# FoX attention: scaling by one over the row sums moved from the probabilities to the gate

## The chip, the cores and the metric

The kernel runs on one core of a Trainium2 chip. The metric is the device time of one execution in microseconds (us), where lower is better. One core has five engines that each work through their own list of instructions in order: TensorE (PE; its weight loads are listed as PEld), VectorE (DVE), ScalarE (ACT), GpSimd (POOL) and SyncE (SP, which here only starts DMAs). ACT starts DMAs too.

## The reference, cut to what matters

Two decoder layers on 1024 tokens of width 1024, in float32. Each layer feeds one projection of the normalised input to three mixers. The one that changes is FoX, a causal softmax attention with a forget decay (8 heads of 64), followed by a SiLU gate and a branch projection:

```python
def _fox_attention(q, k, v, log_f):
    c = jnp.cumsum(log_f, axis=1).transpose(0, 2, 1)
    for s0 in range(0, s, Q_BLOCK):                       # Q_BLOCK = 128
        logits = einsum('bhqd,bhkd->bhqk', q[s0:s1], k[:s1]) * scale
        logits = logits + c[:, :, s0:s1, None] - c[:, :, None, :s1]
        p = jax.nn.softmax(jnp.where(_causal_mask(s0, s1), logits, -jnp.inf), axis=-1)
        outs.append(jnp.einsum('bhqk,bhkd->bhqd', p, v[:, :, :s1]))
...
    y_fox = _fox_attention(...) * jax.nn.silu(fg)
    y_diff = _diff_attention(...) * jax.nn.silu(dg)       # 4 heads, two softmax maps each
    y_conv = cb * _short_conv(cc * cx, conv_w) * jax.nn.silu(cg)
    m = (gates[:, :, 0] * (y_fox @ w_fox) + gates[:, :, 1] * (y_diff @ w_diff)
         + gates[:, :, 2] * (y_conv @ w_conv))
    return x + _rmsnorm(m @ w_o, post_g)
```

## The kernel before, in words

A layer is a row of stages. Projections for the convolution and for most gates come first and keep TensorE full. Then come the attention windows: four FoX pairs of heads, then four differential heads. Each window has attention units as its main work and a list of "fills" beside it (`PLAN`): projections for later heads (tile F on TensorE), gates, and in the last two windows the preparation of the FoX output (`y_prep`, four chunks of 128 rows) and the first three chunks of the branch projection (`merge_br`, "br"). The merge and the output projection follow.

A FoX unit is one head and two query blocks of 128 (`fox_unit`). Stage 1 computes negated logits on TensorE into tile S (L783, L784, with the causal guard L787). DVE adds the decay row cB and finds the minimum (L847, written as ISA in the order and as CUSTOM_DVE in the trace). ACT takes the exponential and its row sum (L854). DVE takes one over the sum (L857) and multiplies the whole probability block by it (L858). Stage 2 (`pv_group`) transposes the probabilities on TensorE into tile T (L174), ACT copies the upper part to tile pt (L821), DVE subtracts for the lower part (L822), and TensorE accumulates P V in tile O (L893, L894). ACT and DVE evict O (L903, L900), and a DMA writes it to the DRAM tensor `of`. Stage 1 of a unit is issued one unit ahead of stage 2.

`y_prep` loads a chunk of attention output o and of gates g, multiplies them on DVE (L1038), and splits the product yf into an upper part on ACT (L1043) and a lower part on POOL (L1044). The branch product reads yf on TensorE (L351 to L353).

What the other engines do after a step is put into the program by an estimated clock (`Clock.later`), and a list scheduler with its own cost model then fixes each engine's order, all but SP's, which follows the program. Large SBUF tiles come from one pool of 41 blocks (`blk`); an SP load into a block waits until the block is free, and everything behind it in SP's queue waits with it.

Of the kernel before, what the change touches and what calls it, by code (L numbers as in the profile page):

```python
# [11 lines left out]
F32 = mybir.dt.float32  # L12
# [4 lines left out]
ALU = mybir.AluOpType  # L17
# [3 lines left out]
S = 1024  # L21
D = 1024
P = 128
HD = 64
EPS = 1e-6
# [9 lines left out]
# order of the query blocks (pairs) of a head, and of the FoX heads (pairs)  # L35
G_ORDER = (1, 2, 3, 0)
FOX_ORDER = (2, 3, 0, 1)
# work on the tensor engine that runs beside each attention pair or head
# [12 lines left out]
# weights of the attention's steps when work beside it is spread between them  # L51
W1F, W2F, W1D, W2D = 0.188, 1.324, 0.31, 1.574
# PSUM banks: logits, transposes, outputs, work beside the attention
# [3 lines left out]
def mm_us(n):  # L57
    """Time of a pass of n columns through the tensor engine."""
    return max(n, 128) * 0.000417


class Clock:
    """Estimated time of the tensor engine. What the other engines do after one of its steps is emitted
    when its turn would come, beside later steps, so that no engine's queue waits on an early entry."""
# [57 lines left out]
def interleave(main, main_cost, fill, fill_cost):  # L122
    """Emit the steps of main with those of fill spread evenly between them."""
# [12 lines left out]
class Trunk:  # L136
# [35 lines left out]
    def transpose(self, out, x):  # L172
        """One block of 128 x 128, through the tensor engine."""
        self.nc.tensor.transpose(out, x, self.ident)  # L174
# [88 lines left out]
    def emit_load(self, key, kt, nco, eng):  # L263
        """DMA one weight tile [P, kt*nco] and split it into hi + lo float32r parts."""
# [18 lines left out]
    def load_w(self, key, kt, nco, eng="gpsimd"):  # L283
        """The next weight tile; the loads of the tiles after it are issued ahead of its use."""
# [19 lines left out]
    def emit_pair(self, l, i0, i1):  # L304
        """DMA two 128-column weight chunks, b1j and b2j their upper and lower halves, and form the split
        operands of a Strassen-Winograd step: b11, b21 | b12 - b11 (t1), b21 - t2 (t4) |
        b22 - t1 (t2), b22 - b12 (t3) | b22."""
# [38 lines left out]
    def mm3(self, ps, pairs, start=True, stop=True):  # L346
        """Accumulate the products of split operands: lo*hi + hi*lo + hi*hi for each k tile."""
# [7 lines left out]
    def proj_g(self, w, h):  # L355
        """One 128-column chunk of the input projection, transposed, for token half h."""
# [18 lines left out]
    # ------------------------------------------------------------------ norm  # L375
    def rstd(self, ss, scale):
        """(ss * scale + EPS) ** -0.5 per partition."""
# [9 lines left out]
    def hk(self, h, k, o=0, n=512):  # L387
        """Tokens o..o+n of a half of hT, 128-row tile k: hi and lo."""
        return [t[:, k % 2, o:o + n] for t in self.hT[h][k // 2]]

    def norm_rows(self, xs, gB, hT, tb0, step):
        """rmsnorm of blocks of 128 tokens (rows of the tiles xs), transposed and split into hT."""
# [40 lines left out]
    # ------------------------------------------------------------------ Strassen-Winograd  # L433
    def build_s(self, L):
        """Sums of the quadrants of h (tokens x features), split: s1 = a21 + a22, s2 = s1 - a11,
        s3 = a11 - a21, s4 = a12 - s2. a21 itself waits in DRAM meanwhile."""
# [46 lines left out]
    def strassen(self, L, c0, c1, use, uv=None):  # L483
        """Two chunks of the input projection, transposed, with seven products in place of eight.
        use(j, h, x, ps, own): chunk j, token half h is x + ps; x may be overwritten if own."""
# [19 lines left out]
    def plain(self, L, jobs):  # L505
        """Chunks of the input projection, transposed, [(chunk, use)]; the first token half of three
        comes before the second."""
# [8 lines left out]
    def total(self, x, ps, own):  # L516
        """x + ps in SBUF, or ps as it is."""
# [6 lines left out]
    # ------------------------------------------------------------------ conv  # L524
    def conv_pair(self, L, c, nplain):
        """Chunks c, c + 1 of the convolution branch; the first nplain projections without Strassen."""
# [785 lines left out]
```

## Time and profile before

| Quantity | Value |
|---|---|
| Time, three runs | 2569.18, 2570.14 (median), 2570.54 us |
| The profiled execution, first to last instruction | 2573.8 us |
| TensorE busy | 2439.4 us, 95% of the span |
| VectorE busy | 1699.8 us, 66% |
| ScalarE busy | 1109.0 us, 43% |
| GpSimd busy | 838.9 us, 33% |
| FoX windows, layer 0 and layer 1 | 587 to 845 us and 1868 to 2126 us |

The profile is of one execution. A wait in it is put down to the instruction that ended last before the waiting one started. Idle time matters where it is TensorE that idles. In the windows view the numbers behind an engine are its busy time and, in brackets, its instructions.

### The profile page before, as it was taken

What the parts mean: (1) busy time and instruction counts of PE and PEld (TensorE: products, weight loads), DVE (VectorE), ACT (ScalarE), POOL (GpSimd) and SP (SyncE); (2) the same over time, 40 slices, a digit from 0 to 9 for tenths busy, and PEclk for the clock granted to TensorE, in tenths of its full rate; (3) what the DMA queues carried; (4) which work ended last, traced back from release to release, by engine and by line L of the source; (5) the groups of instructions that cost most, each with busy time, mean ns of one, the idle gap of its engine ahead of it and who ended that gap; (6) DMA issues with size and microseconds to landing.
All of it is one profiled execution on the core that took longest, in us unless ns stands there. A gap on an engine that the chain in (4) does not pass through costs nothing. (4 is left out here: it accounts for less than half of the span.)

```text
span 2573.8 us, 35788 instructions
## 1 busy us (share of the span) xinstructions
PE 2439.4 (95%) x13104; PEld 2051.8 (80%) x13104; DVE 1699.8 (66%) x3017; ACT 1109.0 (43%) x2282; POOL 838.9 (33%) x605
## 2 busy tenths in 40 slices
PE   7899999999999999899997999999999999989998
PEld 6677888888978778778976778888888787877798
DVE  6976464447687777767578654344486878777664
ACT  4224333336554554543433232233365545555333
POOL 1566334421112222361025652344211122232600
PEclk9899999999999999999998999999999999999999
DMA  4012223332222222563521122233321222225534
GB/s 167 33 50 95 92 96 111 107 132 70 63 69 68 63 87 64 169 220 129 194 90 41 50 95 89 75 117 130 93 80 53 69 68 75 82 70 186 202 119 180
DMA packets 111808, 260.35 MB, mean 101 GB/s; under 512 B 15744, under 2 KB 40576, under 8 KB 111632
## 3 DMA queue, kind: packets, MB, share of 16 engines
q1 hardware_dynamic: 56304, 183.33, 20.7%
q10 hardware_dynamic: 55328, 74.73, 9.4%
q8 instruction: 104, 1.70, 0.3%
q14 instruction: 72, 0.59, 0.1%
HBM read 183.48 MB, written 55.64 MB: 93 GB/s over the span
## 5 line engine op out<-in xcount | busy, mean ns | idle before, releaser
L279 POOL TENSOR_TENSOR wlo<-wraw,whi 128x1024 fp32r<-128x1024 f32 (+2 forms) x93 | 198.5, 2135 | 628.1 <-ACT whi L276 442.3
L351 PE MATMUL F<-ht,wlo 128*128 128x512 f32 x792 | 331.1, 418 | 0.0
L353 PE MATMUL F<-ht,whi 128*128 128x512 f32 x792 | 318.5, 402 | 0.0
L352 PE MATMUL F<-ht,whi 128*128 128x512 f32 x792 | 317.0, 400 | 0.0
L319 POOL TENSOR_TENSOR wlo<-sw,whi 128x512 fp32r<-128x512 f32 x160 | 224.6, 1414 | 228.6 <-ACT whi L318 203.1
L319 POOL TENSOR_TENSOR wlo<-wraw,whi 128x1024 fp32r<-128x1024 f32 x80 | 159.3, 1992 | 188.1 <-ACT whi L318 187.9
L318 ACT CAST whi<-sw 128x512 fp32r<-128x512 f32 x160 | 96.1, 619 | 245.6 <-DVE sw L321 106.1
L353 PEld LDWEIGHTS F<-ht,whi 128*128 128x128 f32 x792 | 150.8, 190 | 30.6
L276 ACT CAST whi<-wraw 128x1024 fp32r<-128x1024 f32 (+2 forms) x126 | 118.0, 939 | 129.8 <-PE F L353 41.9
L822 DVE TENSOR_TENSOR pt<-T,pt 128x512 fp32r<-128x512 f32 (+1 forms) x240 | 147.4, 632 | 37.4 <-ACT pt L821 35.7
L351 PEld LDWEIGHTS F<-ht,wlo 128*128 128x128 f32 x792 | 152.3, 192 | 24.2
L352 PEld LDWEIGHTS F<-ht,whi 128*128 128x128 f32 x792 | 151.5, 191 | 24.5
L821 ACT CAST pt<-T 128x512 fp32r<-128x512 f32 (+1 forms) x240 | 125.1, 544 | 91.3 <-PE T L174 66.1
L783 PE MATMUL S<-qk,qk 128*128 128x512 f32 (+2 forms) x384 | 141.7, 369 | 23.0 <-ACT p L922 21.1
L174 PE MATMUL T<-ident,p 128*128 128x128 f32 x864 | 135.3, 277 | 11.5 <-DVE p L858 6.6
L922 ACT ACTIVATE p<-S,sm 128x512 f32<-128x512 f32 (+2 forms) x192 | 110.5, 582 | 70.2 <-DVE sm L918 35.4
L916 DVE TENSOR_REDUCE sm<-S 128x1 f32<-128x512 f32 (+2 forms) x192 | 104.5, 551 | 48.5 <-PE S L787 29.6
L784 PE MATMUL S<-qk,sw 128*128 128x512 f32 (+2 forms) x384 | 131.8, 348 | 0.0
L318 ACT CAST whi<-wraw 128x1024 fp32r<-128x1024 f32 x80 | 66.8, 834 | 146.0 <-PE S L353 43.7
L351 PE MATMUL F<-whi,ht 128*128 128x256 f32 (+1 forms) x416 | 121.9, 293 | 4.2 <-DVE vd L373 4.2
L854 ACT ACTIVATE p<-p,sm 128x384 f32<-128x384 f32 (+7 forms) x128 | 99.5, 777 | 54.9 <-DVE sm L847 41.5
L321 DVE TENSOR_TENSOR sw<-wraw,sw 128x512 f32<-128x512 f32 x80 | 69.1, 863 | 81.3 <-POOL wlo L319 80.7
(390 smaller groups left out, 7249.2 us busy)
## 6 DMA issues: line engine op xcount, KB each, us to landing
wraw<-wt SPq DMA_DIRECT2D x128, 512.0 KB
mg<-tmp ACTq DMA_DIRECT2D x64, 256.0 KB
sw<-qk ACTq DMA_DIRECT2D x256, 64.0 KB
g<-mg SPq DMA_DIRECT2D x32, 512.0 KB
wraw<-wo SPq DMA_DIRECT2D x32, 512.0 KB
x<-x SPq DMA_DIRECT2D x24, 512.0 KB
wraw<-wbr SPq DMA_DIRECT2D x48, 256.0 KB
m<-tmp ACTq DMA_DIRECT2D x32, 256.0 KB
```

The lines of the kernel that those rows point to most:

```text
L174: self.nc.tensor.transpose(out, x, self.ident)
L276: nc.scalar.copy(hi, raw)
L279: getattr(nc, eng).tensor_tensor(out=lo, in0=raw, in1=hi.bitcast(F32), op=ALU.subtract)
L318: nc.scalar.copy(w[0][:, o], f)
L319: nc.gpsimd.tensor_tensor(out=w[1][:, o], in0=f, in1=w[0][:, o].bitcast(F32), op=ALU.subtract)
L351: nc.tensor.matmul(ps, wl, xh, start=start and i == 0, stop=False)
L352: nc.tensor.matmul(ps, wh, xl, start=False, stop=False)
L353: nc.tensor.matmul(ps, wh, xh, start=False, stop=stop and i == n - 1)
L783: nc.tensor.matmul(ps[:, :wp], q[:, i * P:(i + 1) * P], k[:, c0:c0 + wp], start=True, stop=False)
L784: nc.tensor.matmul(ps[:, :wp], qsw[:, (i % 2) * P:(i % 2) * P + P], k[:, c0:c0 + wp], start=False, stop=not last)
L821: self.clock.later(0.1, lambda: nc.scalar.copy(hi, T[:, n0:]))
L822: done = self.clock.later(0.6, lambda: nc.vector.tensor_tensor(out=lo, in0=T[:, n0:], in1=hi.bitcast(F32), op=ALU.subtract))
```

## The change

The FoX exponentials are no longer multiplied by one over their sum. L858 goes; the reciprocal writes one column of a tile `rl` (16 columns for a pair of heads) and nothing in stage 2 waits for it, since `done` now holds the exponential. When a pair's last unit is done, `sums_out` transposes `rl` on TensorE, copies it on ACT and writes 16 rows to the DRAM tensor `rs`. `y_prep` loads these rows spread over 64 partitions each into a new block `rb` (two DMAs for a chunk, between those of o and g) and multiplies o by it on POOL, ahead of the DVE multiplication with g.

```diff
-    def softmax(self, chunks, n, pr, cb, done):
+    def softmax(self, chunks, n, pr, cb, rl, done):
...
         def norm():
-            nc.vector.reciprocal(out=st[:, 2:3], in_=st[:, 2:3])
-            nc.vector.tensor_scalar(out=pr[:, :n], in0=pr[:, :n], scalar1=st[:, 2:3], scalar2=None, op0=ALU.mult)
+            nc.vector.reciprocal(out=rl, in_=st[:, 2:3])
...
         later(0.0, least)
-        later(t, exp)
-        done.append(later(2 * t + 0.2, norm))
+        done.append(later(t, exp))
+        later(2 * t + 0.2, norm)
...
+            if g == G_ORDER[0] and e == 0:
+                L.rl[p] = self.sm(16, "rl")
...
-                self.softmax(chunks, n, pr, cb, done)
+                self.softmax(chunks, n, pr, cb, L.rl[p][:, 8 * e + i:8 * e + i + 1], done)
...
+            if g == G_ORDER[-1] and e == 1:
+                self.clock.later(0.5, lambda: self.sums_out(L, p))
...
+    def sums_out(self, L, p):
+
+        nc = self.nc
+        T = self.pT()
+        self.transpose(T[0:16, 0:P], L.rl[p])
+        r = self.tmp((P, P))
+        nc.scalar.copy(r[0:16], T[0:16, 0:P])
+        nc.scalar.dma_start(L.rs[16 * p:16 * p + 16], r[0:16])
...
         nc.sync.dma_start(o, L.o[kind][c])
+        if kind == "f":
+            rb = self.blk([P, S], F32, "rb")
+            rows = L.rs.rearrange("(h t) q -> h (t q)", t=8)
+            for e in range(2):
+                nc.sync.dma_start(rb[e * 64:e * 64 + 64], rows[2 * c + e:2 * c + e + 1].to_broadcast([64, S]))
         nc.sync.dma_start(g, L.g[kind + "g"][c])
...
             o1, g1, hi, lo = (t[:, h * 512:h * 512 + 512] for t in (o, g, *y[:2]))
+            if kind == "f":
+                nc.gpsimd.tensor_tensor(out=o1, in0=o1, in1=rb[:, h * 512:h * 512 + 512], op=ALU.mult)
...
+        L.rs, L.rl = dt([64, P], "rs"), {}
```

The scheduler places instructions anew. DVE in the first FoX head pair of layer 0, before: p is a probability block, sm holds its minimum and sum, pt the transposed block.

```order
L847 ISA p_4320,sm_4327<-S_4321,cB_4318 128x384
L847 ISA sm_4327 128x1
L847 ISA p_4320,sm_4363<-S_4357,cB_4318 128x512
L847 ISA sm_4363 128x1
L822 TENSOR_TENSOR pt_4344<-T_4345,pt_4344 128x512
L857 RECIPROCAL sm_4327<-sm_4327 128x1
L822 TENSOR_TENSOR pt_4350<-T_4351,pt_4350 128x384
L858 TENSOR_SCALAR p_4320<-p_4320,sm_4327 128x384
L699 SCALAR_TENSOR_TENSOR qk_4276<-F_4280,qk_4276 64x512
L857 RECIPROCAL sm_4363<-sm_4363 128x1
L858 TENSOR_SCALAR p_4320<-p_4320,sm_4363 128x512
```

The same place of DVE in the changed kernel, where lines are numbered one higher:

```order
L848 ISA p_4322,sm_4329<-S_4323,cB_4320 128x384
L848 ISA sm_4329 128x1
L848 ISA p_4322,sm_4362<-S_4356,cB_4320 128x512
L848 ISA sm_4362 128x1
L822 TENSOR_TENSOR pt_4343<-T_4344,pt_4343 128x512
L858 RECIPROCAL rl_4300<-sm_4329 128x1
L822 TENSOR_TENSOR pt_4349<-T_4350,pt_4349 128x384
L699 SCALAR_TENSOR_TENSOR qk_4277<-F_4281,qk_4277 64x512
L858 RECIPROCAL rl_4300<-sm_4362 128x1
L848 ISA p_4392,sm_4404<-S_4394,cB_4301 128x384
```

The two scalings are gone; the reciprocals stand where they stood, between the same pt subtractions.

TensorE at the same place, before: the seven transposes of one unit (T) and the logits of the next block (S).

```order
L174 MATMUL T_4345<-ident,p_4306 128x128
L783 MATMUL S_4357<-qk_4130,qk_4128 128x512
L784 MATMUL S_4357<-qk_4130,sw_4301 128x512
L787 LDWEIGHTS identb
L787 MATMUL S_4357<-trib,identb 128x128
L174 MATMUL T_4345<-ident,p_4306 128x128 x3
L174 MATMUL T_4351<-ident,p_4306 128x128 x3
L351 MATMUL F_4364<-ht_107,wlo_4124 128x512
```

TensorE there in the changed kernel:

```order
L174 MATMUL T_4344<-ident,p_4308 128x128 x4
L174 MATMUL T_4350<-ident,p_4308 128x128 x3
L783 MATMUL S_4356<-qk_4131,qk_4129 128x512
L784 MATMUL S_4356<-qk_4131,sw_4303 128x512
L787 LDWEIGHTS identb
L787 MATMUL S_4356<-trib,identb 128x128
L351 MATMUL F_4363<-ht_107,wlo_4125 128x512
```

All seven transposes now stand ahead of the logits; six of them stood behind.

TensorE in the third differential window of layer 0, before, where the first branch product begins (F_9858, from yf); T_9816 and T_9822 transpose p of a later unit.

```order
L787 MATMUL S_9761<-trib,identb 128x128
L783 MATMUL S_9789<-qk_8864,qk_8862 128x512
L784 MATMUL S_9789<-qk_8864,sw_9780 128x512
L174 MATMUL T_9816<-ident,p_9613 128x128
L174 MATMUL T_9822<-ident,p_9613 128x128
L353 MATMUL F_9731<-ht_121,whi_9232 128x512
L351 MATMUL F_9731<-ht_121,wlo_9233 128x512
L352 MATMUL F_9731<-ht_122,whi_9232 128x512
L353 MATMUL F_9731<-ht_121,whi_9232 128x512
L351 MATMUL F_9858<-yf_9228,wlo_9417 128x512
L352 MATMUL F_9858<-yf_9229,whi_9416 128x512
```

The end of the same first half of the branch product (F_9839) in the changed kernel; yf_9572 is the last of the four chunks:

```order
L353 MATMUL F_9839<-yf_9540,whi_9387 128x512
L351 MATMUL F_9839<-yf_9572,wlo_9388 128x512
L352 MATMUL F_9839<-yf_9573,whi_9387 128x512
L353 MATMUL F_9839<-yf_9572,whi_9387 128x512
L783 MATMUL S_9672<-qk_8826,qk_8824 128x256
L784 MATMUL S_9672<-qk_8826,sw_9589 128x256
L787 LDWEIGHTS identb
L787 MATMUL S_9672<-trib,identb 128x128
L783 MATMUL S_9704<-qk_8825,qk_8823 128x512
L784 MATMUL S_9704<-qk_8825,sw_9589 128x512
L976 MATMUL O_9643<-pt_9644,vd_8369 128x256
```

The logits and the P V of the attention unit that was done before the first branch product (its O_9643 has all its products behind) now come after it, so the branch product has moved forward in TensorE's list, past attention work.

## Rows read from the trace of the kernel before

**Rows 1.** The page: span, busy time of the engines
```profile
span 2573.8 us, 35788 instructions
PE 2439.4 (95%) x13104; PEld 2051.8 (80%) x13104; DVE 1699.8 (66%) x3017; ACT 1109.0 (43%) x2282; POOL 838.9 (33%) x605
```
**Rows 2.** Windows: FoX, y_prep and branch, in both layers (busy us, instructions)
```profile
587.00:845.00 258.00, 246.85 (x1597) 212.96 (x1596) 199.20 (x500) 142.01 (x315) 41.42 (x51) 0.99 0.24 68
1060.00:1145.00 85.00, 77.56 (x389) 61.85 (x388) 67.61 (x126) 44.41 (x108) 43.11 (x34) 0.98 0.58 206
1868.00:2126.00 258.00, 245.88 (x1596) 212.78 (x1596) 200.82 (x502) 142.60 (x317) 40.31 (x47) 0.99 0.24 68
```
**Rows 3.** Waits of PEld, 587 to 845 us: total us, times, longest
```profile
PEld O L893 <- DVE pt L822: 8.6, 11, 2.4
PEld T L174 <- DVE p L858: 6.0, 11, 1.9
PEld O L893 <- POOL pt L815: 1.8, 1, 1.8
PEld S L783 <- DVE sm L847: 1.5, 1, 1.5
```
**Rows 4.** Waits of PEld, 1868 to 2126 us
```profile
PEld O L893 <- DVE pt L822: 8.1, 10, 2.4
PEld T L174 <- DVE p L858: 7.4, 11, 2.1
```
**Rows 5.** Lines of DVE, 587 to 845 us: busy, mean ns | idle before, releaser
```profile
L822 DVE TENSOR_TENSOR pt<-T,pt 128x512 fp32r<-128x512 f32 (+1 forms) x79 | 48.8, 633 | 10.1 <-ACT pt L821 9.5
L858 DVE TENSOR_SCALAR p<-p,sm 128x384 f32<-128x384 f32 (+7 forms) x63 | 43.5, 692 | 1.6
L857 DVE RECIPROCAL sm<-sm 128x1 f32<-128x1 f32 x64 | 10.2, 161 | 19.3 <-ACT p L854 18.5
```
**Rows 6.** The page: all transposes of probabilities
```profile
L174 PE MATMUL T<-ident,p 128*128 128x128 f32 x864 | 135.3, 277 | 11.5 <-DVE p L858 6.6
```
**Rows 7.** Lines of POOL, 1000 to 1160 us
```profile
L1044 POOL TENSOR_TENSOR yf<-o,yf 128x512 fp32r<-128x512 f32 x8 | 11.1, 1404 | 28.1 <-ACT yf L1043 28.1
```
**Rows 8.** Timeline of POOL, 1063 to 1074 us: start, us [idle before]
```profile
1063.78 2.52 POOL L1044 TENSOR_TENSOR yf<-o,yf 128x512 fp32r<-128x512 f32 x2 [9.68 <-ACT yf L1043]
1070.29 1.30 POOL L1044 TENSOR_TENSOR yf<-o,yf 128x512 fp32r<-128x512 f32 x1 [4.00 <-ACT yf L1043]
...
1073.06 1.28 POOL L1044 TENSOR_TENSOR yf<-o,yf 128x512 fp32r<-128x512 f32 x1
```
**Rows 9.** Tile yf, 1000 to 1160 us: ns min/median/max, first and last start
```profile
L351 PEld LDWEIGHTS F<-yf,wlo x36: 187/188/330, 1080.8 to 1150.2; 128*128 128x128 f32 x36
```
**Rows 10.** Timeline of SP, last two FoX chunks
```profile
1049.53 0.32 SPq L1032 DMA_DIRECT2D o<-of  x1
...
1056.07 0.42 SPq L1033 DMA_DIRECT2D g<-fg  x1
```
**Rows 11.** Waits of SP, 587 to 1160 us
```profile
SPq L1032 <- DMA tmp<-tmp: 16.2, 1, 16.2
SPq L1032 <- DMA od<-tmp: 15.6, 2, 10.8
```
**Rows 12.** Waits of PEld, 1000 to 1160 us
```profile
PEld T L351 <- POOL wlo L279: 4.3, 1, 4.3
```
**Rows 13.** Timeline of DVE, one entry of y_prep
```profile
1027.91 4.54 DVE L1038 TENSOR_TENSOR o<-o,g 128x512 f32<-128x512 f32 x2
```
**Rows 14.** Timeline of POOL at the same time
```profile
1027.29 2.95 POOL L279 TENSOR_TENSOR wlo<-wraw,whi 128x1024 fp32r<-128x1024 f32 x1 [4.32 <-ACT whi L276]
```
**Rows 15.** Tile o, 1000 to 1160 us: ns min/median/max
```profile
L1038 DVE TENSOR_TENSOR o<-o,g x24: 678/692/2874, 1027.9 to 1136.2; 128x512 f32<-128x512 f32 x24
```

## The prediction, on record before the changed kernel ran

> **What bounds the kernel now.** I read the page first, then the windows, then the waits of the engine that the windows show to be the bound, then the lines of the engine that it waits for. TensorE is busy for 95% of the span [rows 1], so any change that leaves its work alone can win at most the idle rest. In the two FoX windows of 258 us each it is busy for 246.85 and 245.88 us [rows 2]: 11.2 and 12.1 us are open there, about 23 us in all, or 0.9% of the span. The reader should see that DVE, with 199 us of 258, is busy without being the bound.
>
> The waits say what TensorE's stalls hang on. I take those of the weight loads, since a matmul can still look busy while its weights wait. In layer 0, P V waits 8.6 us for the lower half of the transposed probabilities (L822 on DVE), and the transposes wait 6.0 us for the scaling L858; two smaller waits make 3.3 us [rows 3]. Layer 1 has 8.1 and 7.4 us [rows 4]. Together 16.7 us of waits on L822 and 13.4 us on L858, 30.1 us in both layers. It is more than the idle time of the windows, because modelled matmul ends cover a part; it is my upper bound.
>
> **What the change removes.** In 258 us of FoX, L858 runs 63 times at 692 ns, which is 43.5 of DVE's 199.2 us [rows 5]. The change takes 128 of them out of the kernel and keeps the reciprocals (161 ns). DVE's busy time in such a window becomes about 199.2 - 43.5 = 155.7 us, 60% in place of 77%.
>
> First term, the transposes. They now wait for ACT's exponential and not for reciprocal and scaling after it: the chain is shorter by 0.161 + 0.692 = 0.85 us. The 22 waits average 13.4 / 22 = 0.61 us and the longest are 1.9 and 2.1 us [rows 3, 4]; one of average length vanishes, and the longest keep 1.1 and 1.3 us. Against this, the new order puts seven transposes ahead of the next logits where six stood behind, so a part of the time won is spent by asking earlier. Bounds: 0 if the scheduler spends all of it, 13.4 us if none. I leave 3.0 us of waits, since the longest two alone keep 2.4: gain 10.4 us.
>
> Second term, P V. Its chain (transpose, ACT copy, L822 of 633 ns) keeps its length; what shrinks is the time that L822 spends behind scalings in DVE's list. Not all of the wait is that: DVE is itself idle for 9.5 us in a window until the copy has come, and 18.5 us until an exponential has come for the reciprocal [rows 5], which still stands between the same two subtractions. Bounds 0 and 16.7 us. I take half, 8.3 us, as DVE's load falls by a fifth and only waits behind scalings fall.
>
> Gain in FoX: 10.4 + 8.3 = 18.7 us.
>
> **What it adds.** Eight transposes of the sums, four in a layer. One on TensorE is 277 ns [rows 6], so 8 x 0.277 = 2.2 us, counted whole because TensorE is the bound (0 if each falls into an idle gap). Their eight small copies and writes lie on ACT, which works 142 of 258 us in the window [rows 2]; 116 us idle hide them, and uncovered they could delay an exponential by about one copy each. The FoX window ends at 845 us and the loads of [rows 10] are issued some 200 us later, so the way through DRAM itself waits for nobody.
>
> The gate is the dear place. In each layer POOL gets eight multiplications on 128 x 512, which the trace shows there at 1.404 us with two inputs of that size [rows 7], 11.2 us in a layer, 22.5 us in all. POOL has the room: 43 of 85 us are busy [rows 2], and yf alone waited 28.1 us for ACT [rows 7]. Only the last chunk counts. Its two subtractions on POOL start at 1070.29 and 1073.06, with 4.00 us idle ahead of them [rows 8], and the first branch product loads its weights at 1080.8 [rows 9]. That is 1080.8 - 1074.3 = 6.5 us of cover. The chain of the last chunk gets longer by its pair of multiplications, 2 x 1.404 = 2.8 us, and by whatever its rows `rb` wait for. The order, though, brings the branch product forward past attention work, so I do not count on the cover and charge 2.8 us for each layer, 5.6 us. Bounds: 0 if the cover holds, 22.5 us if every added multiplication reaches TensorE. The nearest row is one wait of 4.3 us for a POOL result in the same stretch [rows 12]; 2.8 lies near it.
>
> The eight row loads of a layer go into SP's list between o and g, and each chunk asks for one block more. Queued behind are g, the weights `wraw` and the later loads of the merge. The loads of the last two chunks are issued from 1049.53 to 1056.07 [rows 10], the last some 14 us ahead of its result's use on POOL at 1070 [rows 8]; that cover hides a short wait for a block and not a long one, see the second rival.
>
> **A rule to weigh here.** The trace has a pair of DVE multiplications in `y_prep` that took 4.54 us [rows 13], where one has a median of 692 ns [rows 15]; a POOL subtraction had started 0.62 us earlier and ran 2.95 us [rows 14]. The Trainium skill ("SBUF — State Buffer", section "Who interferes with whom") says that a DVE instruction with two SBUF inputs and a POOL instruction that reads SBUF exclude one another for the whole length of the one that came first. By it every added POOL multiplication can hold DVE. The row agrees in kind: the pair lost 4.54 - 1.38 = 3.2 us. The price by the one and by the other is the third rival's.
>
> **The sum.** -18.7 + 2.2 + 5.6 = -10.9 us. The profiled execution took 2573.8 us [rows 1], 3.7 us over the median of 2570.14; I take the difference off the median: 2559 us.
>
> **The rivals.**
>
> *The waits only change their name.* The scheduler asks for the transposes earlier, and they wait for ACT's exponential; DVE still stands at the reciprocal until the exponential has come. For it speak the 18.5 us at L857 [rows 5] and the moved transposes; against it, that 44 us less work on DVE must leave something. A third of the gain stays: -6 + 2.2 + 5.6 = about +2, or 2572 us, no change.
>
> *The gate's loads become a wait of TensorE (slower).* `rb` needs one block more for a chunk, from a pool in which o already waited 16.2 us once and 15.6 us in two waits [rows 11]. One such wait of 16.2 us on the last chunk, less 6.5 us of cover, leaves 9.7 us; with the 2.8 us on POOL, 12.5 us a layer, 25 in both. It decides from the point where the last yf comes more than 6.5 us later. The moved branch product speaks for it, as attention work now stands behind it in TensorE's list and stops too; against it, the 14 us between load and use. In sum: -18.7 + 2.2 + 25 = +8.5, 2579 us.
>
> *DVE and POOL shut one another out (slower).* Each of the 16 added multiplications holds a DVE instruction for its 1.404 us, and attention's minimum and subtraction stand behind it: 22.5 in place of 5.6 us. The 4.54 us entry [rows 13] speaks for it; against it, that one wait in such a window is seen to be that long while POOL runs 34 instructions there [rows 2]. -18.7 + 2.2 + 22.5 = +6, 2576 us. That is the result by the rule on the Trainium skill's page above, if all of it reaches TensorE.
>
> *All FoX waits go.* The two big waits vanish whole and the gate's cover holds: -30.1 + 2.2 = -28, 2542 us. For it speaks that both hang on DVE; against it, that the copy and the exponential on ACT stay.
>
> **How the numbers follow.** Forecast 0.60 (alone 2550 to 2566), same waits under another name 0.14, gate loads 0.10, shut out 0.06, all waits gone 0.10. What a measurement of this kernel can tell from no change is 0.2%, 5.1 us: faster is below 2565.0, slower above 2575.3. Faster: nearly all of the forecast's 0.60 (0.58) and 0.10, 0.68. Same: 0.14, the forecast's rest and a part of the third rival's, 0.18. Slower: 0.14. For 8 in 10 the range runs from 2543, the case of all waits gone, to 2577, between the two slower ones: about 0.07 is left out below and 0.1 above.
>
> **What would show it.** In the FoX windows, DVE should be near 156 us busy; the weight loads' wait on L858 should be gone, with 2 to 4 us in both layers on the exponential in its place; the wait of P V on the subtraction near 8 us in both layers; TensorE idle near 14 us in place of 23. In `y_prep`, POOL's multiplications should take about 1.4 us and the first branch product should wait under 4 us. The prediction is wrong if the wait of P V stays at 16 us (then DVE's load was not its cause), if the transposes wait as long for ACT as they did for DVE, or if the first branch product waits over 7 us for POOL or for a load.

## The result and the profile after

The changed kernel takes 2550.84 us (median of four runs, 2547.05 to 2552.70) where the kernel before takes 2569.94 beside it: a ratio of 0.9922, 95% interval 0.9908 to 0.9936. That is faster by 0.78%: 20.0 us by the ratio, 19.1 us by the two medians. The forecast was 10.9 us. The profiled execution spans 2545.2 us and took 2547.05.

The page of the changed kernel, for [rows 1]:

```profile
span 2545.2 us, 35790 instructions
...
PE 2427.9 (95%) x13112; PEld 2043.0 (80%) x13112; DVE 1620.5 (64%) x2889; ACT 1109.7 (44%) x2290; POOL 859.8 (34%) x621
```

DVE lost 79 us of work, POOL gained 21. TensorE is still 95% busy, and its busy time fell by only 11.5 us, so that most of the gain has to lie in its waits. The same three windows as [rows 2] (us; busy time and count of PE, PEld, DVE, ACT, POOL; granted clock, DMA share, GB/s), FoX of layer 0, the gate, FoX of layer 1:

```profile
583.00:830.00 247.00, 246.11 (x1632) 215.88 (x1630) 162.21 (x443) 145.61 (x323) 43.52 (x52) 1.00 0.25 72
...
1050.00:1140.00 90.00, 77.72 (x360) 60.20 (x359) 61.00 (x110) 40.36 (x96) 50.88 (x41) 0.94 0.58 204
```

```profile
1849.00:2096.00 247.00, 245.65 (x1627) 215.37 (x1625) 161.25 (x441) 144.84 (x323) 43.16 (x52) 1.00 0.25 72
```

In 247 us TensorE does more instructions than before in 258, and is idle for 0.9 and 1.4 us where it was for 11.2 and 12.1 [rows 2]. Its weight loads' waits there, layer 0 first (total us, times, longest), for [rows 3, 4]:

```profile
PEld O L895 <- issue: 1.7, 7, 0.4
...
PEld O L895 <- DVE pt L822: 0.4, 1, 0.4
PEld T L174 <- ACT tmp L918: 0.4, 1, 0.4
```

```profile
PEld O L895 <- DVE pt L822: 1.2, 2, 0.8
```

Of 16.7 us for P V on L822, 1.6 are left (1.7 us a layer, where the profile names no cause, were 0.8 before); of 13.4 us for the transposes of probabilities nothing, and no wait for ACT's exponential took their place. The 0.4 us on `tmp` L918 is the one wait that the sums brought in this layer: a transpose of probabilities waited for the copy of the sums. DVE in the FoX window of layer 0 (busy, mean ns | idle before, releaser), for [rows 5]:

```profile
L822 DVE TENSOR_TENSOR pt<-T,pt 128x512 fp32r<-128x512 f32 (+1 forms) x80 | 49.5, 634 | 15.3 <-ACT pt L821 14.6
...
L858 DVE RECIPROCAL rl<-sm 128x1 f32<-128x1 f32 x64 | 10.2, 161 | 22.5 <-ACT p L855 21.9
```

The subtraction's duration is unchanged, and DVE now stands idle ahead of it for 15.3 us, not 10.1: it comes early.

Below, two stretches are measured in every trace. *FoX* runs from the first product of queries and keys of a layer (S, L783) to the first P V product of the differential heads. *Gate* runs from there to the first product with `yd`, and holds the differential attention, `y_prep` and the FoX branch.

| Kernel | FoX, layers 0 and 1 | Gate, layers 0 and 1 | All four less before's | Ratio of times, 95% interval |
|---|---|---|---|---|
| before | 269.9, 270.4 | 294.1, 293.5 | | 1 |
| changed | 254.5, 255.0 | 300.6, 297.7 | -20.1 | 0.9922 (0.9908 to 0.9936) |
| a: FoX part alone | 254.4, 257.4 | 293.9, 293.3 | -28.9 | 0.9897 (0.9881 to 0.9914) |
| b: gate part, scaling kept | 265.9, 264.4 | 299.3, 300.5 | +2.2 | 1.0010 (1.0000 to 1.0019) |
| c: scaling off the chain | 265.9, 264.6 | 299.3, 300.4 | +2.2 | 1.0013 (1.0002 to 1.0025) |
| e: small scaling on the chain | 262.2, 261.0 | 302.8, 297.6 | -4.3 | 0.9974 (0.9961 to 0.9987) |
| g: rows without a block | 254.5, 255.4 | 297.9, 302.8 | -17.3 | 0.9923 (0.9907 to 0.9939) |
| d: gate ahead of rows | 254.5, 255.3 | 303.6, 302.9 | -11.6 | 0.9925 (0.9901 to 0.9950) |
| i: rows on DVE | 254.5, 255.2 | 300.4, 299.6 | -18.2 | 0.9906 (0.9889 to 0.9924) |
| j: rows by one DMA | 254.5, 254.5 | 317.3, 314.6 | +12.9 | 1.0042 (1.0030 to 1.0053) |
| k: loads alone | 254.5, 255.1 | 296.8, 300.4 | -21.1 | 0.9915 (0.9902 to 0.9929) |
| m: multiplication alone | 254.6, 255.1 | 295.7, 296.7 | -25.9 | 0.9902 (0.9889 to 0.9916) |
| n: loads from GpSimd's queue | 254.4, 257.5 | 299.8, 300.0 | -16.2 | 0.9918 (0.9902 to 0.9933) |
| p: as n, no block | 254.8, 255.4 | 298.9, 298.9 | -20.0 | 0.9920 (0.9906 to 0.9933) |

The stretches agree with the times: 0.9922 of 2570 us is 20.0 us less, and the four stretches together are 20.1 us shorter, FoX by 30.8 and the gate longer by 10.7. That they agree so closely is luck: in the versions below the two differ by up to 8 us (d). The spans of the two profiles differ by more, 28.6 us. The other 8.5 us lie outside these stretches, in projections that the change leaves alone (the layer-0 start is 4.1 us earlier, the way to layer 1 4.4 us shorter); versions with a ratio of 0.99 have them at either length, so I don't count them. A stretch is from one execution, and at the gate this matters: g, with TensorE's and DVE's instructions in the changed kernel's order, is 2.7 us shorter there in layer 0 and 5.1 us longer in layer 1. So a few us at the gate, in one layer, mean little.

### The profile page after: what moved, and what is told of

Same layout as the page of the kernel before. It is cut to its first block, busy times and chain, and to the rows that moved or that the text cites. A ratio compares the mean times of both kernels' runs of the same rounds, so it can differ in the third digit from the quotient of the medians.

```text
span 2545.2 us, 35790 instructions
## 1 busy us (share of the span) xinstructions
PE 2427.9 (95%) x13112; PEld 2043.0 (80%) x13112; DVE 1620.5 (64%) x2889; ACT 1109.7 (44%) x2290; POOL 859.8 (34%) x621
## 5 line engine op out<-in xcount | busy, mean ns | idle before, releaser
L822 DVE TENSOR_TENSOR pt<-T,pt 128x512 fp32r<-128x512 f32 (+1 forms) x240 | 147.9, 633 | 47.1 <-ACT pt L821 45.5
L783 PE MATMUL S<-qk,qk 128*128 128x512 f32 (+2 forms) x384 | 141.0, 367 | 20.6 <-ACT p L935 20.5
L174 PE MATMUL T<-ident,p 128*128 128x128 f32 x864 | 129.5, 274 | 3.4 <-DVE p L946 3.2
```

The source lines that it names most:

```text
L783: nc.tensor.matmul(ps[:, :wp], q[:, i * P:(i + 1) * P], k[:, c0:c0 + wp], start=True, stop=False)
L822: done = self.clock.later(0.6, lambda: nc.vector.tensor_tensor(out=lo, in0=T[:, n0:], in1=hi.bitcast(F32), op=ALU.subtract))
```

## Experiments in FoX: load or chain

The prediction gave FoX two causes, the chain in front of the transposes and DVE's load in front of the subtraction L822. Version **a** does the FoX part alone:

```
-            rb = self.blk([P, S], F32, "rb")            # and its two loads
-                nc.gpsimd.tensor_tensor(out=o1, in0=o1, in1=rb[...], op=ALU.mult)
```

Its FoX output is not scaled by the sums.

> The changed kernel without its gate part: the row loads rb and the POOL multiplications are left out, so the FoX output stays unscaled; the sums are still transposed and written. Theory 1 (the FoX windows give about 31 us, the gate takes about 11 us back): 2539 us, the last two differential windows as in before. Rival (the gate costs nothing, and 19 us is all that FoX gives): 2551 us, like the changed kernel.

Measured: 0.9897, 26.5 us less (of 2570), nearer to the first theory. The gate is as before, FoX as in the changed kernel but for one place in layer 1: P V waited once for 2.5 us there, and TensorE's clock was granted at 0.80 and 0.63 in the six microseconds behind it (2061 to 2067 us). The whole gain, and more, comes from FoX.

Version **b** keeps the scaling where it was, and so the chain and the load, and adds the rest (FoX is scaled twice):

```
+            nc.vector.tensor_scalar(out=pr[:, :n], in0=pr[:, :n], scalar1=rl, scalar2=None, op0=ALU.mult)
-        done.append(later(t, exp))
-        later(2 * t + 0.2, norm)
+        later(t, exp)
+        done.append(later(2 * t + 0.2, norm))
```

> The gate part alone: probabilities are scaled on DVE as in before, and the gate multiplies by one over the sum a second time. Theory 1: the gate costs about 11 us by itself, 2581 us, FoX windows as long as in before, DVE standing near 6 us at the gate multiplication of the last chunk in each layer. Rival (the loss appears only together with the faster FoX): 2570 to 2573 us.

Version **c** keeps DVE's load alone: the scaling is done into a tile that nobody reads, and the transposes wait for the exponential only.

```
+            nc.vector.tensor_scalar(out=self.junk[:, :n], in0=pr[:, :n], scalar1=rl, scalar2=None, op0=ALU.mult)
```

> The changed kernel plus the old DVE scaling of each probability block into a tile that nobody reads: DVE has its 128 scalings back, but the transposes do not wait for them. Theory load (DVE's queue made P V wait): most of the 16 us on L822 and a part of the rest return, 2565 to 2572 us. Theory chain (waiting for reciprocal and scaling was the cost): at most 5 us return, 2551 to 2556 us.

Measured: 1.0010 and 1.0013 (2572.66 and 2571.71 us); c is where the theory of load put it. b's time is where the rival put it, but for another reason: its gate costs 12.2 us in both layers, as the first theory said, and its FoX, which that theory left as before, is 10.0 us shorter. The waits of weight loads in FoX of layer 0, of b and then of c:

```profile
PEld T L174 <- DVE p L859: 7.3, 10, 2.1
...
PEld O L896 <- issue: 3.1, 3, 1.6
PEld S L783 <- DVE sm L848: 2.0, 3, 1.6
PEld O L896 <- DVE pt L822: 1.9, 7, 0.4
```

```profile
PEld O L897 <- issue: 6.9, 8, 2.0
PEld S L784 <- DVE sm L849: 3.5, 2, 2.1
PEld O L897 <- POOL pt L816: 1.9, 1, 1.9
PEld O L897 <- DVE pt L823: 1.7, 5, 0.5
...
PEld T L174 <- ACT p L856: 0.7, 2, 0.4
```

This is the decisive pair. In b the transposes wait 7.3 us for the scaling. In c they wait 0.7 us for the exponential and no more for a scaling, and the stretch is as long: 265.9 and 264.6 us against 265.9 and 264.4. What the transposes no longer waited went to P V ("issue" is a wait that the profile can't name) and to S, which waits for the minimum L849 of DVE. With the scaling kept on DVE, the shorter chain is worth nothing. Taking the scaling away from c (the changed kernel) is worth 11.4 and 9.6 us, and nearly all those waits go together. So it was DVE's pace that FoX waited for, and the wait merely stood at one of its results or another. One thing goes with each such step: the scheduler orders the engines anew, and some 200 of this stretch's 1666 TensorE instructions stand elsewhere in c than in b, and as many elsewhere than in the changed kernel. No version holds that order fixed.

Version **e** was to put the chain back without the load, by a scaling of every 128th column in place:

```
+            nc.vector.tensor_scalar(out=pr[:, :n:128], in0=pr[:, :n:128], scalar1=rl, scalar2=None, op0=ALU.mult)
...                                                      # and `done` waits for it, as in b
```

> The changed kernel with the transposes again behind DVE: after the reciprocal DVE scales one column in 128 of the block, so the dependence is that of before but almost none of its DVE time. Those columns are scaled twice in the result. Theory load: 2552 to 2557 us, as DVE stays free; only about 13 us of transposes' waits could return and most do not. Theory chain: 2564 to 2572 us.

Measured: 0.9974. FoX is 7.7 and 6.0 us longer than in the changed kernel, between the two theories, and the reason is in its line of DVE (FoX of layer 0):

```profile
L859 DVE TENSOR_SCALAR p<-p,rl 128x3 f32<-128x3 f32 (+7 forms) x62 | 27.2, 439 | 1.6
```

The experiment wasn't what it was to be. The small scaling has a median of 231 ns but a mean of 439, so that 27.2 us of the load came back with the chain. It doesn't tell them apart, and whether the chain costs something when DVE is free isn't shown: no run has the one without the other.

Why a scaling of a few columns can take so long, the timeline of e shows (POOL, then DVE):

```profile
705.92 2.39 POOL L279 TENSOR_TENSOR wlo<-wraw,whi 128x1024 fp32r<-128x1024 f32 x1 [13.57 <-issue]
```

```profile
706.63 1.95 DVE L859 TENSOR_SCALAR p<-p,rl 128x3 f32<-128x3 f32 x1
```

It began while a POOL instruction ran and ended 0.3 us after that one. In both FoX stretches of e, 14 of the 128 scalings took at least 0.3 us more than the median of their size. All 14 began while POOL was at work, and only 2 of the other 114 did. The full scalings of before, b and c show the same: 16, 13 and 13 of 128 are that long, all but one in each beginning while POOL was at work (that one within 5 ns of a POOL instruction's start), and 0, 3 and 2 of the shorter ones. Over the medians they lost 23.5, 19.4 and 21.3 us in both layers, those of e 21.9 us. So POOL held them up, and "DVE's load" here has two parts: the scalings' regular time and these holds of up to 2.6 us each.

The holds lie where TensorE waits. Here are all weight loads' waits of over 1 us in the two FoX stretches; "behind a hold" means that a DVE instruction that took at least 0.3 us more than its median, a scaling in all but a few cases, ran during the wait or in the 1 us ahead of it. In before such places make up 68 of 540 us.

| Kernel | Scalings held | Waits over 1 us | Of these behind a hold | FoX longer than the changed kernel's |
|---|---|---|---|---|
| before | 16 | 13 | 13, 24.2 us | 30.8 us |
| b | 13 | 12 | 12, 19.3 us | 20.8 us |
| c | 13 | 12 | 12, 20.2 us | 21.0 us |
| e | 14 | 7 | 6, 10.7 us | 13.7 us |
| changed | no scaling left | 0 | 0 | |

So the waits behind held instructions nearly make up what FoX loses in b and c, and most of it in before and e; little is left for the scalings' regular time. It also says why c is as slow as b: the same holds stop TensorE, at the next product in place of the transposes. This is read from the traces. No run keeps the scalings' time and takes the holds away, or has the order of the changed kernel with them.

One part of the FoX gain is neither chain nor load. Version b has chain and load as before, and yet its FoX is 4.0 and 6.0 us shorter than before's; its P V waits for L822 are 1.9 us where they were 8.6 [rows 3], while those without a named cause grew from 0.8 to 3.1. Its holds by POOL are shorter by 4.1 us in both layers. What b changes there is the order of TensorE's work, with the transposes of the sums in it, and the tile of the reciprocals. A part of it is the clock. Before has, in both layers at the same place, a stretch at a lower granted clock (layer 0 and 1):

```profile
776.00:779.00 3.00, 3.00 (x17) 2.90 (x16) 1.68 (x7) 0.96 (x2) 0.00 (x0) 0.57 0.12 27
779.00:782.00 3.00, 3.00 (x17) 2.61 (x15) 1.27 (x5) 1.51 (x3) 0.00 (x0) 0.87 0.38 112
2056.00:2059.00 3.00, 3.00 (x17) 2.90 (x16) 1.43 (x6) 1.51 (x3) 0.00 (x0) 0.57 0.14 30
```

What came ahead of it, in the timeline of before's weight loads:

```profile
775.69 0.19 PEld L893 LDWEIGHTS O<-pt,vf 128*128 128x128 f32 x1 [2.37 <-DVE pt L822]
```

And what came ahead of that, on POOL and then on DVE (the first scaling shows what this size takes when POOL is idle):

```profile
771.73 2.39 POOL L279 TENSOR_TENSOR wlo<-wraw,whi 128x1024 fp32r<-128x1024 f32 x1 [12.31 <-ACT whi L276]
```

```profile
768.48 0.42 DVE L858 TENSOR_SCALAR p<-p,sm 128x384 f32<-128x384 f32 x1
...
772.49 2.55 DVE L858 TENSOR_SCALAR p<-p,sm 128x384 f32<-128x384 f32 x1
774.96 1.14 DVE L822 TENSOR_TENSOR pt<-T,pt 128x512 fp32r<-128x512 f32 x2
```

POOL held the scaling, the subtraction stood behind it, and P V waited 2.37 us for the subtraction. After this wait, the longest for P V, TensorE went on at the lower level, 1.2 GHz, for a while. 0.43 of 3 us and 0.13 of 3 us are 1.7 us lost a layer. Neither b, c nor the changed kernel has such a stretch in FoX; a has one, behind its one wait of 2.5 us. So a wait can cost more than its length. The other 2 to 4 us of b are shorter waits; which change of order shortened them is open.

## Experiments at the gate: loads or multiplication

The gate took 5.4 us more a layer in the mean (300.6 and 297.7 against 294.1 and 293.5), nearly twice what was charged. Here is how the last FoX chunk goes in the changed kernel. SP (start, us, engine, line), the loads of the last chunk:

```profile
1045.46 2.08 SPq L1050 DMA_DIRECT2D rb<-rs  x2
1049.70 0.33 SPq L1051 DMA_DIRECT2D g<-fg  x1
```

POOL, DVE, ACT and TensorE, each with the idle time ahead of it in brackets:

```profile
1053.28 2.55 POOL L1057 TENSOR_TENSOR o<-o,rb 128x512 f32<-128x512 f32 x2 [1.87 <-DMA rb<-rs]
```

```profile
1055.60 1.37 DVE L1058 TENSOR_TENSOR o<-o,g 128x512 f32<-128x512 f32 x2 [6.62 <-issue]
...
1059.66 0.42 DVE L929 TENSOR_REDUCE sm<-S 128x1 f32<-128x256 f32 x1 [2.68 <-PE S L787]
```

```profile
1056.41 0.62 ACT L1063 CAST yf<-o 128x512 fp32r<-128x512 f32 x1 [7.10 <-DVE o L1058]
```

```profile
1057.08 0.50 PE L351 MATMUL F<-yf,wlo 128*128 128x512 f32 x1 [1.15 <-ACT yf L1063]
...
1058.42 0.50 PE L352 MATMUL F<-yf,whi 128*128 128x512 f32 x1 [0.84 <-POOL yf L1064]
```

The branch product itself loses only 2.0 us. But DVE and ACT, which work in order, stand at the gate for 6.6 and 7.1 us, and the differential heads' softmax, which is theirs too, stands behind. TensorE fills the time with projections and the branch product; the next logits (S) stand behind that product in its list, so DVE, done with the gate, waits another 2.68 us for them. Attention comes later by all that, and it shows in the waits of weight loads for it, 990 to 1140 us:

```profile
PEld S L783 <- ACT p L935: 8.9, 8, 3.2
...
PEld O L977 <- DVE pt L822: 3.1, 4, 1.5
```

In version a these are 6.7 and 0.8 us.

Four theories of what makes this dear were tried in four versions: the block for `rb` (**g** loads the rows into the tile that `yf`'s lower half goes into later), the number of DMAs (**j** loads both heads' rows by one DMA in place of two), POOL (**i** multiplies on DVE), and the place in the list (**d** loads `g` ahead and lets DVE gate before POOL multiplies).

```
g   -            rb = self.blk([P, S], F32, "rb")
    +            rb = y[1].bitcast(F32)                         # y is now taken ahead of the loads
j   -            for e in range(2):
    -                nc.sync.dma_start(rb[e * 64:e * 64 + 64], rows[2 * c + e:2 * c + e + 1].to_broadcast([64, S]))
    +            nc.sync.dma_start(rb, rows[2 * c:2 * c + 2].unsqueeze(1).to_broadcast([2, 64, S]))
i   -                nc.gpsimd.tensor_tensor(out=o1, in0=o1, in1=rb[...], op=ALU.mult)
    +                later(0.0, lambda o1=o1, r1=rb[...]: nc.vector.tensor_tensor(out=o1, in0=o1, in1=r1, op=ALU.mult))
d   +        nc.sync.dma_start(g, L.g[kind + "g"][c])            # ahead of the rows
    +                later(0.0, ... nc.gpsimd.tensor_tensor(out=o1, in0=o1, in1=r1, op=ALU.mult))   # behind mul
```

> The changed kernel with the rows rb loaded into the tile of yf's lower part, which is written only later: the gate needs no block more. Theory block (the extra block makes loads wait): the gate's loss of about 7 us goes, 2544 to 2546 us. Theory queue (two more DMAs per chunk ahead of g make it late, whatever they are loaded into): 2549 to 2552 us. Theory POOL (its multiplications lengthen the chain): 2549 to 2552 us.

> The changed kernel with the rows of both heads of a chunk loaded by one DMA in place of two; block, bytes and POOL's multiplications as they are. Theory queue: about half of the 7 us goes, 2546 to 2548 us, and g of the last chunk is issued earlier. Theories block and POOL: no change, 2549 to 2552 us.

> The changed kernel with the multiplication by the rows on DVE in place of POOL (16 times about 0.69 us). Theory POOL: the chain of the last chunk is 1.3 us or more shorter and POOL no longer shuts DVE out: 2544 to 2547 us. Theories queue and block: 2549 to 2553 us, since g and rb come as late as before.

> The changed kernel with the order turned round: g is loaded ahead of the rows, DVE multiplies by the gate first, and POOL by the rows after it. Theory queue in its narrow form (DVE stands 6.6 us at the gate multiplication because g is issued behind rb): the stand goes, 2545 to 2547 us. If only the whole chain counts: 2549 to 2552 us, with the last yf as late.

Measured: 0.9923, 1.0042, 0.9906, 0.9925 (of 2570: 2550, 2581, 2546, 2551 us). The block is not it (g as the changed kernel), nor is the place in the list (d the same, with a longer gate in its trace). In d DVE no longer stands at the last gate multiplication, but for 7.12 us behind it, for logits that come after the branch product in TensorE's list: the stand has moved. For i the ratio is lower, where the theory of POOL put it, but its interval, 0.9889 to 0.9924, holds the changed kernel's, and its gate is as long in the trace: a gain isn't shown. The miss is j, which is slower than before. POOL and DVE at the gate of j:

```profile
1052.95 2.48 POOL L1056 TENSOR_TENSOR o<-o,rb 128x512 f32<-128x512 f32 x2 [11.19 <-issue]
...
1068.28 2.48 POOL L1056 TENSOR_TENSOR o<-o,rb 128x512 f32<-128x512 f32 x2 [8.80 <-DMA rb<-rs]
```

```profile
1054.25 2.33 DVE L1057 TENSOR_TENSOR o<-o,g 128x512 f32<-128x512 f32 x2 [6.12 <-POOL o L1056]
...
1070.01 1.90 DVE L1057 TENSOR_TENSOR o<-o,g 128x512 f32<-128x512 f32 x2 [8.66 <-POOL o L1056]
```

```profile
1057.17 0.47 PE L174 MATMUL T<-ident,p 128*128 128x128 f32 x1 [6.78 <-DVE p L946]
```

Its last row load was issued earlier than in the changed kernel, at 1039.08 and not 1045.46, and the one before it at about the same time (timeline of SP):

```profile
1036.06 0.51 SPq L1049 DMA_DIRECT2D rb<-rs  x1
...
1039.08 0.51 SPq L1049 DMA_DIRECT2D rb<-rs  x1
```

Yet their users start at 1052.95 and 1068.28, 15.3 us apart. The windows view of j, where little else is under way:

```profile
1047.50:1052.50 5.00, 2.89 (x15) 2.15 (x13) 0.59 (x3) 1.73 (x6) 0.00 (x0) 1.00 0.14 55
```

A DMA share of 0.14 is about two of the 16 engines (2 / 16 = 0.125). The transfer's slowest dimension has two entries, the heads. The Trainium skill ("DMA: Bandwidth & Descriptors", section "Why a DMA increments its semaphore by 16 and not by 1") says that a transfer is spread over the largest number of engines, up to 16, that divides the slowest dimension of both its sides, which is 2 here; the trace agrees. So j delays the rows, and the price is 17 us a layer above the changed kernel: DVE waits for POOL, the softmax stands behind DVE, and a transpose of a softmax result stops TensorE for 6.78 us. This is the prediction's rival "the gate's loads become a wait of TensorE", made true, if by a slow transfer and not by a wait for a block.

The last four versions take loads and multiplication apart. **k** leaves out the multiplication and keeps the loads; **m** multiplies the FoX output by itself and loads nothing. **n** is i with the loads issued by GpSimd, and **p** is n without the block, where TensorE's order is nearly that of a. k has the changed kernel's order of TensorE and m that of a, so "the loads" below include the order that comes with them.

```
k   -                nc.gpsimd.tensor_tensor(out=o1, in0=o1, in1=rb[...], op=ALU.mult)
m   -            rb = self.blk([P, S], F32, "rb")            # and its two loads
    +                nc.gpsimd.tensor_tensor(out=o1, in0=o1, in1=o1, op=ALU.mult)
n   -                nc.sync.dma_start(rb[...], rows[...])
    +                nc.gpsimd.dma_start(rb[...], rows[...])
p   -            rb = self.blk([P, S], F32, "rb")            # beside n's edit
    +            rb = y[1].bitcast(F32)                         # y is now taken ahead of the loads
```

> The changed kernel with the rows of reciprocals still loaded at the FoX gate, but no multiplication by them (the FoX output stays unscaled). TensorE's instructions stand in the order of the changed kernel. The stretch looked at is from the first differential P V product to the first product of the next branch's output: 294 us per layer before the change and without loads and multiplication, 298 to 301 us with both. If the loads cost (SyncE's queue, the waits that its DMAs share with ScalarE's, the order of TensorE's work that comes with them): 297 to 301 us per layer, ratio to the kernel before 0.991 to 0.993. If the multiplication costs: 293 to 295 us, ratio 0.989 to 0.9905.

> The changed kernel without the loads of the rows; GpSimd multiplies the FoX output by itself in their place, two 128x512 multiplications per chunk as in the changed kernel (the FoX output is not scaled by the sums). TensorE's instructions stand in the order that they have without loads and multiplication. If the loads cost: 293 to 295 us from the first differential P V product to the first product of the next branch, ratio 0.989 to 0.9905. If the multiplication costs (GpSimd in the way of the lower weights and of VectorE): 297 to 301 us, ratio 0.991 to 0.993.

> The rows are loaded by DMAs that GpSimd issues, so that SyncE's queue holds what it held before the change; the multiplication by the rows is done by VectorE, as in the version with 0.9906. If what the loads cost lies in SyncE's queue and in the DMA semaphores that its loads share with ScalarE's stores: 293 to 296 us in the stretch at the gate, ratio 0.9895 to 0.991. If it is the transfer of 2 MB more per layer by itself (the DMA engines are 0.58 busy at the gate): 298 to 301 us, ratio 0.991 to 0.993. If GpSimd, which works in order, waits at its issues for the rows or for the tile and holds back the lower weights: 300 to 306 us, ratio 0.993 to 0.996.

> As the version with the loads on GpSimd's queue, and the rows land in the tile that the lower part of the gate's result is written to later, so that no further tile is taken. TensorE's instructions at the gate then stand nearly as they do without the loads. If the order of TensorE's work, which the loads moved, is what costs: 293 to 296 us in the stretch at the gate and below the version that differs only in the tile by 1 to 4 us, ratio 0.9893 to 0.9908. If the order doesn't matter: equal to that version within 1 us per layer.

Measured: 0.9915, 0.9902, 0.9918, 0.9920 (2548, 2545, 2549, 2549 us). Against a's gate (293.9 and 293.3) the multiplication alone took 1.8 and 3.4 us more a layer, the loads alone 2.9 and 7.1, both together 6.7 and 4.4. They don't add up, and with one trace each they need not. The ratios stand in the same order (0.9897 for a, 0.9902, 0.9915, 0.9922), but neighbours' intervals overlap, and those of a and the changed kernel do by a little, so the cost rests on the stretches: in the ten versions with loads, j aside, a layer's gate takes 296.8 to 303.6 us, in before and a 293.3 to 294.1.

The stand of DVE at the last chunk comes with the loads: before the last gate multiplication of layer 0, DVE stands 4.0 us in k and not at all in m, and in k and the changed kernel it then waits 2.9 and 2.7 us for logits. In layer 1 of the changed kernel the profile names what it waits for, 5.6 us for the load of `g`, which SP issues behind the rows.

Of n and p none is better than the changed kernel: another queue, no block and nearly a's order of TensorE don't help. p's gate is within 1.1 us of n's, so nothing speaks for the order that differs between them. n came out where the theory of the transfer by itself put it, but that doesn't show it: VectorE multiplies by the rows in n and p and is 7 to 11 us longer busy at the gate than in a, and no run has this multiplication without the loads. In p a new wait has come, 9.8 us of ACT for POOL's `mf`. Why the loads cost as much from GpSimd's queue, where DVE waits only 1.3 to 1.8 us for them, stays open.

m shows one thing more. The gate stretch of layer 0 in a, then in m:

```profile
841.20:1135.10 293.90, 273.80 (x1489) 225.27 (x1489) 225.10 (x457) 154.23 (x387) 103.52 (x85) 0.98 0.38 123
```

```profile
839.30:1135.00 295.70, 273.79 (x1490) 225.31 (x1490) 227.88 (x457) 154.09 (x387) 113.66 (x93) 0.98 0.38 122
```

DVE does the same 457 instructions in both, and in m they take 2.8 us longer (4.8 in layer 1). POOL does 10.1 and 7.9 us more there. So DVE and POOL do hold each other up, as the third rival had it, but for a quarter to three fifths of POOL's added time and not for all of it, and the layers lose 1.8 and 3.4 us where the rival charged 11. The rule that the rival took from the Trainium skill ("SBUF — State Buffer", section "Who interferes with whom") agrees with this in kind.

## Why the prediction was right, and where it was not

Faster was right, and 2550.84 lies at the lower edge of the forecast's own range (2550 to 2566).

*First term, transposes 10.4 us.* The waits on L858 went, all 13.4 us and not 10.4, and the 2 to 4 us on the exponential didn't come. As a cause the term isn't borne out: c takes the scaling off this chain, keeps it on DVE and gains nothing. That "one of average length vanishes, and the longest keep 1.1 and 1.3 us" went by the mean of 692 ns. The longest waits stood behind scalings that POOL held for about 2 us, and these went whole.

*Second term, P V 8.3 us.* Right in kind, undersized. All of the 21.0 us between c and the changed kernel came with the scalings that left DVE (and the order that the scheduler made of it), and 20.2 us of c's waits stand behind instructions that POOL held. I split one cause over two waits, and halved one, since "DVE is itself idle for 9.5 us in a window until the copy has come". But that idle time was no reason: in the changed kernel it is longer, 14.6 us, and the wait is nearly gone. Idle time elsewhere in a window doesn't say that an engine is early where it is waited for. And I weighed POOL's holds for the added multiplications alone, not for the scalings that the change removes.

*The upper bound.* 30.1 us of waits in FoX stood as the most that could go; 30.8 went. In it are 10.0 us that b gains as well, of which the clock's return is 3.4; no term had either. TensorE's idle time, the 23 us that I gave as the most to win, fell by 21.0 us in the FoX stretches, and its busy time, at modelled ends and at the granted clock, by another 9.8. "All FoX waits go", at 0.10, was what happened in FoX: I gave it too little.

*Transposes of the sums, 2.2 us.* Each takes 0.272 us in the trace, so eight make 2.2 us. They are part of a FoX window with 0.9 us of idle time in 247, so they can hardly be hidden there, but no run has FoX without them.

*DVE's load.* 155.7 us of 258 predicted; 162.2 of 247, as more of the program fits into the window.

*The gate, 5.6 us.* The multiplication was priced rightly: 1.29 us each in the median, 2.8 us a layer charged, 1.8 and 3.4 in the traces when alone. The step that failed is the cover of the loads, which I let cost nothing ("hides a short wait for a block and not a long one"). They took 2.9 and 7.1 us in the two layers when alone, 10.0 by the stretches and 4.6 by the ratios (0.9915 less 0.9897, not clear of noise). Together with the multiplication it is 11.1 us in both layers by the stretches, 6.4 us by the ratios (0.9922 less 0.9897, each with an interval of 4 us either way). I looked at the branch product, which in fact waited 2.0 us, under the 4 that I had named; what lost time was the attention beside it, through DVE and ACT. The rival "gate's loads" named that ("attention work now stands behind it in TensorE's list and stops too") but by way of a block, and g shows no gain without the block.

So two errors met: by the stretches FoX gave 30.8 us, 14 more than forecast (18.7 less 2.2), and the gate took 10.7, 5 more. That the time fell into the range is partly luck: with the gate as charged, FoX alone would have brought about 2545 us, below it. The rival "waits only change their name" holds for c, where the load stays, and not for the change.

## What to carry to other kernels

When an engine that is busy but not the bound lies in several chains, don't add its waits chain by chain: ask what taking its load away is worth, because a wait that is taken off one chain can show up on the next until the load goes. Look at a line's longest instances and not only at its mean, and at what another engine did when they began. Where operands are brought to an in-order engine that serves two parts of the program, price the standing of the other part, not only that of the consumer. Before two transfers are joined into one, look at its slowest dimension, and at the DMA share in the trace.

## What the runs showed of the hardware that I had not expected

One DMA for two heads' rows ran at a DMA share of 0.14 and 55 GB/s, and its users started 15.3 us apart; the changed kernel has two DMAs per chunk issued at 1045.46 and its user starts at 1053.28, 7.8 us later. A wait of 2.37 us on TensorE was followed by a granted clock of 0.57 and 0.87 for 3 us each, in both layers at the same place. In before's FoX stretches, 16 of 128 DVE scalings took 0.83 to 2.65 us where the medians are 0.29 to 0.75 us by size; POOL was at work, or within 5 ns of it, when each of the 16 began and when none of the others did. A scaling of one to eight columns was held in the same way: it had a median of 231 ns, a mean of 439 and a longest of 2862 ns, so that leaving out most columns saved only 38% of DVE's time for it (27.2 us against 43.5 [rows 5]).
